# Two-layer diffusion backbone: where five modulation columns, the w2 loads and two weight casts of layer 1 stand in the program

## Chip, cores and metric

The kernel runs on one NeuronCore of a Trainium2 chip, in one launch. The metric is the device time of one execution in microseconds (us). Lower is better.

## The reference

A latent stream of 512 rows by 1,024 columns passes two layers; all arithmetic is f32.

```
for i in range(2):
    sh1, sc1, g1, sh2, sc2, g2 = split(silu(c) @ ada_w[i] + ada_b[i], 6)   # 6 vectors of 1024
    h = rms_norm(x, norm1_g[i]) * (1 + sc1) + sh1
    if i == 0:   # latent attention (8 heads) || Fourier mixing
        mix = concat(latent_attention(h @ a_w_in, context), fourier_mix(h @ a_w_in)) @ a_w_out
    else:        # conformer convolution || short gated convolution
        a, gate, sb, scc, sx = split(h @ b_w_in, 5 parts of 512)
        conf = depthwise_conv(a * sigmoid(gate), 31 taps) + bias
        conf = silu(group_layer_norm(conf, 4 groups))
        sc = sb * depthwise_conv(scc * sx, 3 taps)
        mix = concat(conf, sc) @ b_w_out
    x = x + g1 * mix
    h2 = rms_norm(x, norm2_g[i]) * (1 + sc2) + sh2
    x = x + g2 * ((silu(h2 @ w1[i]) * (h2 @ w3[i])) @ w2[i])        # inner width 2816
```

## The kernel before

Activations lie transposed in the on-chip buffer: tiles of 128 channels by 512 rows. A weight tile ("unit") is 128 by 1,024 f32 (512 KB; 448 KB for a part of w2). Every product with a weight is made of three matmuls on TensorE (`mm3`, L117 to L120): high part times high part, high times low, low times high. So a unit takes three steps: a DMA into a buffer `wraw` (three of them, `RB`), a cast to the high part `whi` on ScalarE (L95), and a subtraction that leaves the low part `wlo` (L96) on VectorE, or on GpSimd in layer 1's input projection (`lo_eng=G`). A unit of eight 128-wide blocks is 24 matmuls of 512 columns.

**Modulation columns.** The six vectors per layer are made in columns of 128 values. One column is a 512 KB DMA into a buffer `ada` (two of them, `AB`) and one multiply-and-sum on VectorE (L156 in `ada_tile`; L177 in `AdaJob.reduce`). The columns that are needed later wait in a list `bg` and are taken from it one by one: by `pump` in the plain part of layer 0's feed-forward, and by `pump_ahead` under the windows and the output tiles.

**Layer 0's output projection** is a list of steps between which `weave` spreads given columns.

**Layer 0's feed-forward** (`ffn_blocks(0, ...)`) goes over 22 inner blocks `f` in three segments of 8, 7 and 7 (`SEGS`). The first three blocks are plain (`proj` with `done`); the others are windows of small matmuls (L1212). At the end of each segment stand the output tiles: eight tiles `mt` of the product with w2, with `w2_ahead` for the weights of coming tiles, `pump_ahead` for a few modulation columns, and `add`, which puts the product into the residual (L327). The last segment's output tiles are called the turn here; layer 1's first input weights (`next_srcs`) and its first norm are prepared there. From the end of the plain part on, instructions are issued in the order of the program text. Elsewhere the framework's scheduler sets the order, save where a pair is pinned by `keep_in_program_order`.

**Layer 1's input projection** (`proj(in1, n1_1, done1, lo_eng=G, ..., pinned=3)`) has 20 units. Units 0 to 2 run interleaved, first on the left half of the rows, then on the right, while the norm's right half is prepared (`nrm.s2(1)`, `nrm.s3(1)`, whose last instructions on ScalarE are at L256). Units 3 to 19 follow one by one. `done1` takes each product: a gate's sigmoid on ScalarE (L1524), the product a * sigmoid on VectorE (L1530), and from it the 31-tap convolution of 128 channels. Its taps run on VectorE (L1474, on an accumulator in PSUM that ScalarE starts at L1471) and the last few as a scaling on ScalarE (L1478) with a sum on GpSimd (L1480). Each engine issues in order, so a weight's cast can stand behind a tap.

Of the kernel before, what the change touches and what calls it, by code (L numbers as in the profile page):

```python
# [60 lines left out]
def tile_dit(  # L61
# [914 lines left out]
    g1s = ada_jobs(0, "g1", 16, 8)  # L976
    s2s = ada_jobs(0, "s2", 24, 16)
    weave(pre, (g1s + s2s)[:SA0])
    weave(asteps, (g1s + s2s)[SA0:SA1])
# [23 lines left out]
    for x in END_ORDER.split():  # L1003
# [3 lines left out]
        else:  # L1007
            last.append(end[x])
    weave(last, (g1s + s2s)[SA1:])
    head0 = head_units(0)  # L1010
# [6 lines left out]
    def proj(srcs, nrm, done, first=3, lo_eng=None, head=(), mid=None, pinned=0):  # L1017
# [11 lines left out]
        for k in range(KT):  # L1029
            for u in range(first):  # L1030
                mm(u, k, 0, HS)
            if k == PH[0]:
                nrm.s1(1)
            if k == PH[1]:
                nrm.s2(1)
                nrm.s3(1)
        for u in range(first):
            for k in range(KT):
                mm(u, k, HS, S)
            done(u, pss[u])  # L1040
        for i in range(first, n):
            wh, wl = unit(srcs[i], D, lo_eng, i < first + pinned)
            if i == n - 1 and mid is not None:
                mid()
            p = ps()
            for k in range(KT):
                c = slice(k * P, (k + 1) * P)
                mm3(p, wh[:, c], wl[:, c], hh(k), hl(k), k == 0, k == KT - 1)
            done(i, p)
# [5 lines left out]
    def ffn_blocks(l, nrm, head, sq_next=None, make_next=None, next_srcs=(), next_head=None):  # L1055
# [30 lines left out]
        def done(i, p):  # L1086
# [11 lines left out]
            split(d[:, 0, :], d[:, 1, :], g)  # L1098
            if f < NPL - 1:
                pump(2)  # L1100
# [225 lines left out]
        for a, n in SEGS:  # L1326
# [3 lines left out]
            def w2src(mt):  # L1330
                return w2[l, mt, :, a:a + n, :]
# [32 lines left out]
            def w2_ahead(mt):  # L1364
                if mt + 3 < KT:
                    raw2.append(raw_unit(w2src(mt + 3), n * P))
                if mt + 2 < KT:
                    u = hilo()
                    split(u[0][:, :n * P], u[1][:, :n * P], raw2.pop(0)[:, :n * P])
                    wu.append(u)  # L1370
# [11 lines left out]
            for mt in range(full):  # L1382
# [4 lines left out]
                if not last and mt == KT - 2:  # L1387
                    run_prep(pn[4:])
                pump_ahead(((2, 1, 1, 1, 2, 0, 0, 0) if turn else (2, 2, 2, 2, 1 + (a == 0), 0, 0, 0))[mt])
                if turn and 0 < mt <= 3:  # L1390
# [39 lines left out]
    head1 = []  # L1430
    bg.extend(ada_jobs(0, "g2", 40, 8))
    bg.extend(ada_jobs(1, "s1", 0, 16))
# [121 lines left out]

    proj(in1, n1_1, done1, lo_eng=G, head=head1, pinned=3)
    g1b = mods[1, "g1"]
# [102 lines left out]
```

## Time and profile before

| | |
|---|---|
| device time, median of 3 runs | 1206.2 us (1205.64 to 1206.95) |
| device time of the profiled execution | 1205.26 us |
| its span in the trace | 1203.4 us |
| TensorE busy, share of the span | 1169.7 us, 97% |
| VectorE busy | 891.8 us, 74% |
| ScalarE busy | 517.8 us, 43% |
| GpSimd busy | 131.8 us, 11% |
| mean granted TensorE clock | 0.991 of full speed |

The span is the time from the first to the last instruction in the trace; the device time has 1.9 us more around it. A share is an average over stages with different limits, so what a change is worth is read in its own stage. In the trace PE is TensorE, PEld its weight load, DVE VectorE, ACT ScalarE, POOL GpSimd, and SP the engine that issues most DMAs; L with a number is a line of the kernel before. Matmuls overlap in the pipeline, so the pace is the distance between two starts, not the duration shown.

### The profile page before, as it was taken

Reading aid. Unit: us, or ns where it says so; the run is one execution under the profiler, and the core shown is the slowest. Engines: PE = TensorE matmul, PEld = TensorE weight load, DVE = VectorE, ACT = ScalarE, POOL = GpSimd, SP = SyncE. Lnnn points to the kernel's source line nnn. Section 1 sums busy time; section 2 is a strip of 40 time slices with the busy share of each in tenths; the row PEclk is TensorE's granted clock in tenths of the full one; section 3 lists DMA queues with packets and bytes.
Section 4 is the critical chain, followed back from the end, with each engine's and each line's share of the span. In section 5 each row is a group of like instructions: output and inputs, shape, how many; then the busy total and the mean of one; then the engine's idle time right before and its main releaser. Section 6 shows DMA issues by size and latency. Waiting matters only on the chain.

```text
span 1203.4 us, 18092 instructions
## 1 busy us (share of the span) xinstructions
PE 1169.7 (97%) x7128; PEld 1008.7 (84%) x7128; DVE 891.8 (74%) x1473; ACT 517.8 (43%) x879; POOL 131.8 (11%) x121
## 2 busy tenths in 40 slices
PE   8999999999999999999999879999999999999998
PEld 6777856569989899879988758878999889989997
DVE  7989877747887688678867779966877468757852
ACT  5545455535643244324433445433644235434530
POOL 1013300000000000000001187300000000000000
PEclk9999999999999999999999889999999999999999
DMA  9872033382478667766576032222068437726432
GB/s 345 300 290 88 1 109 102 108 268 97 135 217 249 233 195 224 219 219 203 159 255 197 18 123 88 80 96 88 28 175 210 123 90 179 210 73 159 113 100 94
DMA packets 56265, 188.34 MB, mean 157 GB/s; under 512 B 6130, under 2 KB 7026, under 8 KB 55923
## 3 DMA queue, kind: packets, MB, share of 16 engines
q1 hardware_dynamic: 51426, 169.88, 42.3%
q0 software_dynamic: 4752, 17.30, 8.5%
q8 instruction: 56, 0.92, 0.3%
q14 instruction: 31, 0.25, 0.1%
HBM read 185.06 MB, written 2.10 MB: 156 GB/s over the span
## 4 chain that ended last, share of the span: by engine, by line
PE 78%; DMA 9%; DVE 7%; ACT 2%; issue 2%; POOL 1%; SPq 0%; ACTq 0%; DVEq 0%; POOLq 0%
PE ps L1212 25%; PE ps L118 13%; PE ps L120 13%; PE ps L119 13%; DMA wraw<-in_w 5%; PE ps L921 2%; DMA ada<-in_ada 2%; PE ps L763 1%; DVE ada L177 1%; PE ps L636 1%; PE ps L926 1%; PE ps L906 1%; DVE s L96 1%; ACT whi L95 1%; PE ps L907 1%
## 5 line engine op out<-in xcount | busy, mean ns | idle before, releaser
L118 PE MATMUL ps<-s,whi 128*128 128x512 f32 (+1 forms) x758 | 283.1, 374 | 11.4 <-ACT whi L95 10.9
L1212 PE MATMUL ps<-s,whi 128*128 128x256 f32 x1584 | 287.4, 283 | 3.2 <-DVE t L1233 3.1
L120 PE MATMUL ps<-s,wlo 128*128 128x512 f32 (+1 forms) x758 | 279.1, 368 | 6.2 <-POOL wlo L96 3.9
L119 PE MATMUL ps<-s,whi 128*128 128x512 f32 (+1 forms) x758 | 278.3, 367 | 0.0
L1212 PEld LDWEIGHTS ps<-s,whi 128*128 128x128 f32 x1584 | 247.7, 192 | 4.7 <-DVE t L1233 3.8
L1212 PE MATMUL ps<-s,wlo 128*128 128x256 f32 x792 | 224.2, 283 | 0.4 <-DVE wlo L96 0.4
L95 ACT CAST whi<-wraw 128x1024 fp32r<-128x1024 f32 (+1 forms) x102 | 102.8, 1013 | 180.6 <-DMA wraw<-in_w 99.7
L118 PEld LDWEIGHTS ps<-s,whi 128*128 128x128 f32 x758 | 144.8, 191 | 37.2 <-ACT whi L95 13.4
L120 PEld LDWEIGHTS ps<-s,wlo 128*128 128x128 f32 x758 | 144.4, 190 | 34.0 <-POOL wlo L96 5.3
L119 PEld LDWEIGHTS ps<-s,whi 128*128 128x128 f32 x758 | 144.8, 191 | 22.8 <-issue 0.7
L1212 PEld LDWEIGHTS ps<-s,wlo 128*128 128x128 f32 x792 | 152.0, 192 | 0.6 <-DVE wlo L96 0.6
L96 DVE TENSOR_TENSOR wlo<-wraw,whi 128x1024 fp32r<-128x1024 f32 (+1 forms) x85 | 99.6, 1171 | 36.9 <-ACT whi L95 35.9
L327 DVE SCALAR_TENSOR_TENSOR x<-ps,m_g,x 128x512 f32<-128x512 f32 (+1 forms) x85 | 56.0, 666 | 79.6 <-PE ps L120 79.6
L95 ACT CAST whi<-s 128x1024 fp32r<-128x1024 f32 x65 | 67.7, 1046 | 73.1 <-PE ps L1212 31.8
L1139 POOL DMA_DIRECT2D s<-in_w x32 | 28.0, 875 | 559.9 <-DVE wlo L96 144.2
L96 DVE TENSOR_TENSOR wlo<-s,whi 128x1024 fp32r<-128x1024 f32 x65 | 78.9, 1221 | 6.3 <-ACT whi L95 4.0
L177 DVE CUSTOM_DVE_ANT_0 ada<-ada,scb,vec 128x1024 f32<-128x1024 f32 x52 | 66.2, 1280 | 11.6 <-DMA ada<-in_ada 11.6
L119 PE MATMUL ps<-s,s 128*128 128x256 f32 (+1 forms) x208 | 63.7, 309 | 0.4 <-DVE s L299 0.4
L120 PE MATMUL ps<-s,s 128*128 128x256 f32 (+1 forms) x208 | 63.2, 306 | 0.0
L118 PE MATMUL ps<-s,s 128*128 128x256 f32 (+1 forms) x208 | 61.3, 309 | 0.1
L1474 DVE SCALAR_TENSOR_TENSOR ps<-s,vec,ps 128x512 f32<-128x512 f32 x78 | 56.2, 751 | 2.1 <-ACT ps L1471 0.9
L1212 PE MATMUL ps<-s,u 128*128 128x256 f32 x396 | 52.9, 283 | 0.0
(285 smaller groups left out, 1903.9 us busy)
## 6 DMA issues: line engine op xcount, KB each, us to landing
ada<-in_ada SPq DMA_DIRECT2D x82, 512.0 KB, 3.9
s<-in_w SPq DMA_DIRECT2D x33, 768.0 KB, 5.7
wraw<-in_w SPq DMA_DIRECT2D x38, 512.0 KB, 4.8
s<-in_w SPq DMA_DIRECT2D x64, 256.0 KB, 4.3
s<-in_w POOLq DMA_DIRECT2D x32, 512.0 KB, 5.6
wraw<-in_w SPq DMA_DIRECT2D x32, 448.0 KB, 4.5
wraw<-in_w_in SPq DMA_DIRECT2D x17, 512.0 KB, 3.5
s<-in_ada SPq DMA_DIRECT2D x16, 512.0 KB, 6.7
```

What stands on the lines that cost most here:

```text
L95: i = A.copy(hi, src)
L96: j = (eng or V).tensor_sub(lo, src, f32(hi))
L118: T.matmul(o, wh, ah, start=start, stop=False)
L119: T.matmul(o, wh, al, start=False, stop=False)
L120: T.matmul(o, wl, ah, start=False, stop=stop)
L177: V.tensor_tensor_reduce(self.raw, self.raw, scb, 1.0, vc("ada_b", self.idx), ALU.mult, ALU.add, accum_out=self.dst)
L327: V.scalar_tensor_tensor(X[m][:, a:b], psum, gcol, X[m][:, a:b], ALU.mult, ALU.add)
L636: T.matmul(p[:, c], fst["fa"][:, g % 2, t, s * P:(s + 1) * P], fst["cs"][:, t, c], start=(t == 0), stop=(t == 3))
L921: T.matmul(p[64 * x:64 * x + 64, :], vh[t][:, 2 * j + x, :], ost["p", 2 * j + x, tp][:, s * S:(s + 1) * S], start=(t == 0), stop=(t == 5))
L1139: G.dma_start(s13, w[:, :D], accum_op=ALU.add)
L1212: T.matmul(o, w, b, start=start and kk == 0 and i == 0, stop=kk == 3 and i == 2, skip_group_check=True)
L1474: V.scalar_tensor_tensor(dst, cp[:, w:w + S], vec[:, o + w:o + w + 1], src, ALU.mult, ALU.add)
```

## The change

Five edits, all between layer 0's output projection and layer 1's input projection.

1. Five of the eight columns of layer 0's `g2` no longer wait in `bg`; `weave` spreads them in layer 0's output projection.
2. In the plain part, `done` takes two columns after block 0 alone, and no longer after block 1.
3. `w2_ahead` asks for the fourth and the fifth w2 unit together at the first output tile, so that each later request stands one tile earlier.
4. In the output tiles of the first two segments `pump_ahead` takes 2, 1, 2, 1, 2 columns in place of 2, 2, 2, 2, 1 (the first segment: 2). The turn's numbers stay.
5. In layer 1's input projection two units (3 and 4) are made right behind the norm, inside the loop over units 0 to 2, and pinned there. Before, units 3, 4 and 5 were pinned at the place of their use.

```
+    g2s = ada_jobs(0, "g2", 40, 8)
...
-    weave(last, (g1s + s2s)[SA1:])
+    weave(last, (g1s + s2s)[SA1:] + g2s[:5])
...
             if k == PH[1]:
                 nrm.s2(1)
                 nrm.s3(1)
+                ahead = [unit(srcs[i], D, lo_eng, True) for i in range(first, first + pinned)]
...
         for i in range(first, n):
-            wh, wl = unit(srcs[i], D, lo_eng, i < first + pinned)
+            wh, wl = ahead.pop(0) if ahead else unit(srcs[i], D, lo_eng)
...
-            if f < NPL - 1:
+            if f == 0:
                 pump(2)
...
             def w2_ahead(mt):
-                if mt + 3 < KT:
-                    raw2.append(raw_unit(w2src(mt + 3), n * P))
+                while 2 < len(raw2) + len(wu) <= mt + 4 and len(raw2) + len(wu) < KT:
+                    raw2.append(raw_unit(w2src(len(raw2) + len(wu)), n * P))
...
-                pump_ahead(((2, 1, 1, 1, 2, 0, 0, 0) if turn else (2, 2, 2, 2, 1 + (a == 0), 0, 0, 0))[mt])
+                pump_ahead(((2, 1, 1, 1, 2, 0, 0, 0) if turn else (2, 1, 2, 1, 2, 0, 0, 0))[mt])
...
-    bg.extend(ada_jobs(0, "g2", 40, 8))
+    bg.extend(g2s[5:])
...
-    proj(in1, n1_1, done1, lo_eng=G, head=head1, pinned=3)
+    proj(in1, n1_1, done1, lo_eng=G, head=head1, pinned=2)
```

The first place is ScalarE behind the norm of layer 1. The last line of L256 is the end of the norm; `t<-ps` is the gate's sigmoid, `ps<-s,vec` starts a convolution, `s<-s,vec` are ScalarE's taps, and `whi_` with `wraw_` is a weight's cast. Before:

```order
L256 ACTIVATE s_994_6170<-t_6322,m_s_2688 128x256
L1524 ACT_TABLE_LOAD
L1524 ACTIVATE t_6386<-ps_6243 128x512
L1471 ACTIVATE ps_6416<-s_1029_6412,vec 128x512
L1478 ACTIVATE s_1031_6417<-s_1029_6412,vec 128x512
L1478 ACTIVATE s_1009_6240<-s_1029_6412,vec 128x512 x2
L1524 ACTIVATE t_6453<-ps_6245 128x512
L95 CAST whi_6462<-wraw_6461 128x1024
L1471 ACTIVATE ps_6496<-s_1037_6492,vec 128x512
L1478 ACTIVATE s_1039_6497<-s_1037_6492,vec 128x512
L1478 ACTIVATE s_1009_6240<-s_1037_6492,vec 128x512 x3
L95 CAST whi_6512<-wraw_6511 128x1024
```

And with the change:

```order
L256 ACTIVATE s_994_6170<-t_6322,m_s_2703 128x256
L95 CAST whi_6327<-wraw_6326 128x1024
L95 CAST whi_6333<-wraw_6332 128x1024
L1526 ACT_TABLE_LOAD
L1526 ACTIVATE t_6398<-ps_6243 128x512
L95 CAST whi_6553<-wraw_6552 128x1024
L1473 ACTIVATE ps_6428<-s_1035_6424,vec 128x512
L1480 ACTIVATE s_1037_6429<-s_1035_6424,vec 128x512
L1480 ACTIVATE s_1009_6240<-s_1035_6424,vec 128x512 x2
L1526 ACTIVATE t_6465<-ps_6245 128x512
L95 CAST whi_6603<-wraw_6602 128x1024
L95 CAST whi_6648<-wraw_6647 128x1024
```

The casts of units 3 and 4 (the first two) now stand ahead of the sigmoid, and that of unit 5 ahead of the first convolution; two lines further on, L1473 starts the second convolution only behind a third cast, `whi_6692`.

The second place is GpSimd in the same stretch, from its last work for the norm (L148) on. Before, the sums of ScalarE's taps (L1480) stood between the low parts of units 3, 4 and 5:

```order
L148 TENSOR_TENSOR r_6278<-ms_6276,nhalf 128x2
L1480 TENSOR_TENSOR s_1031_6417<-s_1031_6417,s_1009_6240 128x512 x2
L96 TENSOR_TENSOR wlo_6463<-wraw_6461,whi_6462 128x1024
L1480 TENSOR_TENSOR s_1039_6497<-s_1039_6497,s_1009_6240 128x512 x3
L96 TENSOR_TENSOR wlo_6513<-wraw_6511,whi_6512 128x1024
```

With the change the same line numbers are two higher (L1482):

```order
L148 TENSOR_TENSOR r_6278<-ms_6276,nhalf 128x2
L96 TENSOR_TENSOR wlo_6328<-wraw_6326,whi_6327 128x1024
L96 TENSOR_TENSOR wlo_6334<-wraw_6332,whi_6333 128x1024
L96 TENSOR_TENSOR wlo_6554<-wraw_6552,whi_6553 128x1024
L1482 TENSOR_TENSOR s_1037_6429<-s_1037_6429,s_1009_6240 128x512 x2
L96 TENSOR_TENSOR wlo_6604<-wraw_6602,whi_6603 128x1024
```

Three low parts now stand ahead of the first sums.

The third place is the DMA issues of SP at the output tiles of the first segment (`wraw` is w2, `ada` a modulation column). Before:

```order
L114 DMA wraw_3692<-in_w 128x1024
L114 DMA wraw_3701<-in_w 128x1024
L174 DMA ada_3709<-in_ada 128x1024
L174 DMA ada_3712<-in_ada 128x1024
L114 DMA wraw_3740<-in_w 128x1024
L174 DMA ada_3748<-in_ada 128x1024
```

And with the change:

```order
L114 DMA wraw_3703<-in_w 128x1024
L114 DMA wraw_3712<-in_w 128x1024
L114 DMA wraw_3714<-in_w 128x1024
L174 DMA ada_3721<-in_ada 128x1024
L174 DMA ada_3725<-in_ada 128x1024
L114 DMA wraw_3753<-in_w 128x1024
L174 DMA ada_3760<-in_ada 128x1024
```

A third w2 load now stands ahead of the first two columns; it goes into the buffer that the preceding unit's split leaves. The turn's issues are moved in the same way.

## Rows read from the trace of the kernel before

**Rows 1.** The page, chain of work that ended last: shares by engine.

```profile
PE 78%; DMA 9%; DVE 7%; ACT 2%; issue 2%; POOL 1%; SPq 0%; ACTq 0%; DVEq 0%; POOLq 0%
```

**Rows 2.** Waits of PE: line, awaited line: us in total, times, longest.

```profile
PE ps L118 <- ACT whi L95: 10.9, 3, 6.0
PE ps L120 <- POOL wlo L96: 3.9, 2, 2.1
```

**Rows 3.** Timeline of PE, layer 1's input projection: start, us, instruction, [idle before].

```profile
682.87 0.79 PE L118 MATMUL ps<-s,whi 128*128 128x512 f32 x1 [3.25 <-ACT whi L95]
...
698.73 0.80 PE L118 MATMUL ps<-s,whi 128*128 128x512 f32 x1 [6.02 <-ACT whi L95]
...
706.42 0.39 PE L118 MATMUL ps<-s,whi 128*128 128x512 f32 x1
...
715.96 0.39 PE L118 MATMUL ps<-s,whi 128*128 128x512 f32 x1
```

**Rows 4.** Windows: stretch, length, busy us by engine, PEclk, DMA share, GB/s.

```profile
247.00:270.00 23.00, 23.00 (x120) 18.01 (x119) 14.73 (x17) 9.89 (x13) 1.06 (x1) 1.00 0.83 268
676.00:690.00 14.00, 8.99 (x44) 7.26 (x43) 9.76 (x13) 5.95 (x8) 4.85 (x3) 0.76 0.12 38
690.00:705.00 15.00, 6.87 (x21) 4.75 (x21) 12.15 (x19) 6.81 (x9) 9.12 (x6) 0.70 0.10 36
679.50:803.40 123.90, 110.38 (x480) 88.77 (x479) 103.74 (x146) 53.36 (x71) 64.28 (x41) 0.93 0.28 94
```

**Rows 5.** Timeline of ACT, layer 1's input projection.

```profile
676.04 1.28 ACT L1524 ACT_TABLE_LOAD   x1 [1.16 <-PE ps L120]
...
681.78 1.03 ACT L95 CAST whi<-wraw 128x1024 fp32r<-128x1024 f32 x1
693.61 0.78 ACT L1471 ACTIVATE ps<-s,vec 128x512 f32<-128x512 f32 x1 [10.79 <-DVE s L1530]
...
697.65 1.03 ACT L95 CAST whi<-wraw 128x1024 fp32r<-128x1024 f32 x1
```

**Rows 6.** Timeline of POOL, the same stretch.

```profile
683.45 2.35 POOL L96 TENSOR_TENSOR wlo<-wraw,whi 128x1024 fp32r<-128x1024 f32 x1
...
699.65 2.36 POOL L96 TENSOR_TENSOR wlo<-wraw,whi 128x1024 fp32r<-128x1024 f32 x1
```

**Rows 7.** Timeline of DVE, from the first convolution to the last product that awaits it.

```profile
679.57 9.46 DVE L1474 SCALAR_TENSOR_TENSOR ps<-s,vec,ps 128x512 f32<-128x512 f32 x12 [0.91 <-ACT ps L1471]
...
714.87 0.69 DVE L1530 TENSOR_TENSOR s6a<-ps,t 128x512 f32<-128x512 f32 x1 [5.43 <-PE ps L120]
...
803.36 0.75 DVE L327 SCALAR_TENSOR_TENSOR x<-ps,m_g,x 128x512 f32<-128x512 f32 x1 [1.18 <-PE ps L120]
```

**Rows 8.** Timeline of DVE and PE, end of the plain part.

```profile
330.59 1.28 DVE L156 CUSTOM_DVE_ANT_0 ada<-ada,scb,vec 128x1024 f32<-128x1024 f32 x1 [1.62 <-DMA ada<-in_ada]
...
333.07 0.39 PE L1212 MATMUL ps<-s,wlo 128*128 128x256 f32 x1 [0.44 <-DVE wlo L96]
...
337.67 0.50 PE L1212 MATMUL ps<-s,whi 128*128 128x256 f32 x2 [1.71 <-DVE t L1233]
```

**Rows 9.** Timeline of PE, output tiles of the first and the second segment.

```profile
424.23 0.50 PE L120 MATMUL ps<-s,wlo 128*128 128x512 f32 x1 [0.53 <-DVE wlo L96]
...
521.68 0.50 PE L120 MATMUL ps<-s,wlo 128*128 128x512 f32 x1 [0.39 <-DVE wlo L96]
```

**Rows 10.** Timelines of SP's queue and PE, the turn.

```profile
622.16 1.53 SPq L174 DMA_DIRECT2D ada<-in_ada  x2
623.79 0.38 SPq L114 DMA_DIRECT2D wraw<-in_w  x1
...
642.88 0.39 PE L118 MATMUL ps<-s,whi 128*128 128x256 f32 x1 [1.60 <-ACT whi L95]
```

**Rows 11.** The page: the columns' group on DVE, and the loads from issue to landing.

```profile
L177 DVE CUSTOM_DVE_ANT_0 ada<-ada,scb,vec 128x1024 f32<-128x1024 f32 x52 | 66.2, 1280 | 11.6 <-DMA ada<-in_ada 11.6
...
ada<-in_ada SPq DMA_DIRECT2D x82, 512.0 KB, 3.9
```

## The prediction

> **What bounds the kernel now.** I read the chain of the work that ended last first: 78% of it is TensorE, the rest is mostly DMA and VectorE [rows 1]. So there is little to win but the places where TensorE stands still, and the next view is the list of TensorE's waits. Its two largest entries belong together: 10.9 us for a weight's high part from ScalarE and 3.9 us for a low part from GpSimd [rows 2]. The timeline puts nearly all of both into layer 1's input projection: TensorE idles 3.25 us ahead of unit 3 and 6.02 us ahead of unit 4 [rows 3].
>
> The waits are not the whole loss there. While TensorE stands, the granted clock falls: 0.76 of full speed over 676 to 690 us and 0.70 over 690 to 705 [rows 4], so that matmuls run at the lower of the two levels (1.2 in place of 2.4 GHz) for some microseconds behind each wait. I measure the whole from end to end. Unit 3's first matmul waits until 682.87 and could have started 3.25 us earlier, at 679.62. At 706.42 stands matmul 13 of unit 4, behind 24 of unit 3 and 12 of unit 4. The pace without a wait is (715.96 - 706.42) / 42 = 0.227 us, the 42 being the matmuls between those two rows [rows 3]. So 36 matmuls need 8.2 us and took 26.8: **18.6 us** are lost.
>
> Why were the weights late? ScalarE's cast of unit 3 came at 681.78, that of unit 4 at 697.65 [rows 5], and GpSimd's low parts at 683.45 and 699.65 [rows 6]. ScalarE is not full: ahead of unit 4's cast it waited 10.79 us at 693.61 to start the second convolution, for VectorE's product [rows 5], which itself needs TensorE's unit 3. It is a ring: TensorE waits for the cast, the cast stands behind a convolution that waits for TensorE.
>
> **The change, part by part.**
>
> *Edit 5, the two casts behind the norm.* ScalarE has 1.16 us of idle time behind the norm, up to 676.04, where it waits for unit 0 [rows 5]. The casts go there: from 674.9 (676.04 less 1.16), 1.03 us each, to 676.9. The sigmoid then starts some 0.8 us late, and with it VectorE's first tap, at 680.4 in place of 679.57 [rows 7]. GpSimd, now without sums ahead, makes a low part in 2.35 us [rows 6]: unit 3's from 675.9 to 678.3, unit 4's to 680.6, unit 5's to 683.0. TensorE needs unit 3 at 679.6, unit 4 at 679.6 + 24 x 0.227 = 685.1, unit 5 at 690.5. None is late, so the ring is cut and up to 18.6 us come back.
>
> What is late next is VectorE. From the first tap to the residual at 803.36 that closes the first step of layer 1's output projection it is busy 103.74 of 123.9 us [rows 4, 7]. If it never waited, it would be there at 680.4 + 103.7 = 784.1; TensorE without the loss is there at 803.36 - 18.6 = 784.8. Both ends coincide, so any wait that VectorE keeps costs TensorE too. One I expect: ScalarE must make three casts ahead of the second convolution's start, the last into a buffer that GpSimd releases with unit 5's low part, at 683.0; a load takes 3.9 us by the nearest row [rows 11] and the cast 1.03, so ScalarE gets on at 688, some 2 us after VectorE could use it. I take **16.0 us** for this edit, 18.6 less 2.6; the bounds are 18.6 and 11 (rival 1).
>
> *Edits 1 and 2.* Block 1's two columns leave the plain part: 2 x 1.28 us of VectorE, and a 1.62 us wait for the second one's load [rows 8]. Right behind them TensorE waits 0.44 and 1.71 us for VectorE [rows 8]; both go, with about 0.35 us of slower restarts behind them (estimated from the 0.50 us of the matmul pair at 337.67 where the usual is 0.40): 2.5 us (bounds 1.5 and 2.5). In exchange five columns, 5 x 1.28 = 6.4 us of VectorE, go into layer 0's output projection. VectorE is busy 14.73 of 23 us there and TensorE 23.00 of 23 [rows 4]: the 8.3 us of idle VectorE time cover them, in pieces, and I cost them at nothing. Their five loads of 512 KB need 9.8 us at that stretch's 268 GB/s, with the DMA engines busy 0.83 [rows 4], so weights may come later; the bound is 2 us, and without any cover 6.4.
>
> *Edits 3 and 4.* Under the output tiles of the first segment TensorE waits once 0.53 us for a low part, and in the second three times 0.39, 0.39 and 0.34; the first of each stands for them [rows 9]. Each leaves 0.17 us of slower pace behind. One column less in the second and the fourth tile gives VectorE 1.28 us [rows 11], and the weights are asked for a tile earlier: I count all back, 0.7 + 1.6 = 2.3 us (lower bound 0).
>
> In the turn the table of columns is the same and only the requests move. There two columns were issued at 622.16 and the w2 load at 623.79, behind them [rows 10]; now a w2 load goes ahead of two columns, and VectorE, in order, reaches the columns first. If a 448 KB load delays them by what it moves at 268 GB/s, about 1.7 us, and part of that is slack, VectorE's loop gets 1 us later; against that stands TensorE's 1.60 us wait for a weight at 642.88 [rows 10], which an earlier request may shorten. I take a loss of 1.0 us (bounds +2.5 and -2.5). The Trainium skill (DMA: Bandwidth & Descriptors, Queues, rings and completion order) says that descriptors of one ring are consumed in ring order, which speaks against asking for w2 first; by it the loss would be the 1.7 us whole, and rows 10 show only issues, no landing order that could decide.
>
> **Sum.** 16.0 + 2.5 - 0 + 2.3 - 1.0 = 19.8 us. The profiled execution took 1205.26 us, its span 1203.4; so 1185.5 us for one like it, and from the median of 1206.2, which is 0.9 us higher, **1186.4 us**.
>
> **Rivals.**
>
> 1. *The convolution becomes the bound.* VectorE has no microsecond to spare by the sum above; the point from which it decides is 2.6 us of waits in all. If GpSimd is slower with three low parts in a row, say 4.7 us each (twice the 2.35 of rows 6), the third buffer is free at 690, its cast ends at 695, and the second convolution starts 7 us later than I count. Edit 5 then gives back 9 to 12 us in place of 16.0, and the time is 1190.5 to 1193.5. For it: VectorE's thin margin. Against it: the low part at 683.45 took 2.35 us while VectorE was in the midst of its taps, and the one at 699.65 took 2.36 [rows 6, 7]. The Trainium skill (SBUF — State Buffer, SBUF: two separate sides) gives it a mechanism: VectorE and GpSimd share a port pair as an exclusive lock when a VectorE instruction reads two operands from this buffer, which the norm's do; those two rows show no such lock beside taps, which read PSUM and one operand.
> 2. *Only unit 3's wait goes.* If a later unit has to wait as unit 4 does now, because its load, asked for only when GpSimd frees a buffer, lands late, half of the loss returns: 6.02 + 2 + some 3 us of low clock, 11 us, so 1197 (1194 to 1203). It decides if a load takes over 13 us: unit 6's buffer is asked for at 678.3 and the unit is needed at 695.9, and the landing is 3.9 us by rows 11. Against it: that margin.
> 3. *Slower.* In each of 15 output tiles with columns (five per segment) the w2 load stands ahead of the columns on SP's queue and itself waits for a buffer. If VectorE's columns came later by a whole load, 3.9 us [rows 11], less the tile's slack, taken as 1.2, each tile would cost 2.7 us: 15 x 2.7 = 40, less the 18.5 of the other places is 21.5 slower, 1228. It decides from 18.5 / 15 = 1.2 us per tile. For it: VectorE already waits 11.6 us for columns in all [rows 11]. Against it: each request moves ahead of a column by one place, and the tiles of the first two segments lose columns.
>
> **How the numbers follow.** The forecast (1182 to 1190) 0.66; rival 1 (1190 to 1194) 0.20; rival 2 (1194 to 1203) 0.09; rival 3 0.04; a better end than all of these 0.01. The range 1182 to 1194 leaves out 0.14; its lower end is all of the 18.6 and the turn's better bound in part (18.6 + 2.5 + 2.3 + 0.5 = 23.9), its upper end rival 1 with the bound of 2 us in layer 0's output projection. This kernel's measurement can tell 0.2%, 2.4 us, from no change. Faster by more 0.94, within it 0.02 (the end of rival 2's tail), slower 0.04.
>
> **What would show it.** Edit 5 right: no idle time of TensorE ahead of units 3 and 4, a granted clock of 1.00 over the whole input projection, casts directly behind L256, and VectorE over 95% busy from its first tap to the close of the output projection's first step, at about 787 in before's count, less what earlier edits gave. Rival 1: the same casts, but TensorE waits for VectorE's mean or merge in the output projection. Rival 2: a wait for ScalarE at unit 5 or later. Edits 1 to 4: no waits like those of rows 8 and 9, and in the turn either a longer wait than 1.60 us (my loss) or a shorter one. Rival 3: more idle VectorE time ended by a column's load, in every tile. The prediction fails most cheaply if VectorE holds up the mean of a convolution, or if layer 0's output projection, which I cost at nothing, starts to wait for its weights.

## The result, and the profile after

The changed kernel takes 1186.34 us (median of 3 runs, 1184.24 to 1187.83) against 1206.2 before: a ratio of 0.983 (95% interval 0.981 to 0.986). The prediction was 1186.4. That the median fits to a tenth is partly luck, as the parts below show; a second set of runs beside the kernel before on another chip gave 1188.35 with the same ratio, 0.983 (0.981 to 0.985). The profiled execution took 1184.24 us, its span 1182.4, 21.0 less than before's.

The chain of the work that ended last now has 84% of TensorE where [rows 1] had 78%:

```profile
PE 84%; DVE 4%; DMA 4%; issue 3%; POOL 2%; ACT 2%; SPq 0%; POOLq 0%; DVEq 0%; ACTq 0%
```

The list of TensorE's waits (line, awaited line: us in total, times, longest) has lost both entries of [rows 2]; the 2.6 us for a cast are the turn's 1.54 and one of 1.04 us in the second segment's tiles. A new one stands near the top, for a merge (L1489) ahead of a convolution's mean:

```profile
PE ps L343 <- ACT crow L134: 3.2, 1, 3.2
PE ps L1503 <- DVE s L1489: 2.8, 1, 2.8
PE ps L118 <- ACT whi L95: 2.6, 2, 1.5
PE ps L120 <- DVE wlo L96: 1.4, 3, 0.6
```

In the timeline of PE, unit 3 (675.59) and unit 4 (681.04) of layer 1's input projection start without any idle time, where [rows 3] had 3.25 and 6.02 us; the distance between the two, 5.45 us, is 24 matmuls at full pace:

```profile
675.59 0.40 PE L118 MATMUL ps<-s,whi 128*128 128x512 f32 x1
...
681.04 0.39 PE L118 MATMUL ps<-s,whi 128*128 128x512 f32 x1
...
716.64 1.12 PE L1503 MATMUL ps<-s,ones 128*128 128x512 f32 x2 [2.80 <-DVE s L1489]
```

The windows (stretch, length, busy us of PE, PEld, DVE, ACT and POOL, PEclk, DMA share, GB/s) show a granted clock of 1.00 where [rows 4] had 0.76 and 0.70. They also show GpSimd busy nearly without a break (41.52 of 45 us over 675 to 720), which no row of before had:

```profile
672.00:686.00 14.00, 14.00 (x78) 12.23 (x77) 8.85 (x13) 12.09 (x16) 13.90 (x7) 1.00 0.41 130
686.00:701.00 15.00, 15.00 (x68) 12.40 (x67) 15.00 (x24) 6.65 (x10) 14.69 (x10) 1.00 0.44 141
675.00:720.00 45.00, 42.20 (x188) 34.40 (x187) 40.17 (x58) 24.65 (x34) 41.52 (x25) 1.00 0.40 132
```

ScalarE's timeline has the two casts right behind the norm (L256), ahead of the table load, where [rows 5] had them at 681.78 and 697.65. The third cast before the second convolution waits 1.45 us for its load, so L1473 starts at 683.61; the last row is for later:

```profile
670.10 0.91 ACT L256 ACTIVATE s<-t,m_s 128x256 fp32r<-128x256 f32 x2 [1.06 <-DVE t L251]
670.91 1.98 ACT L95 CAST whi<-wraw 128x1024 fp32r<-128x1024 f32 x2
672.92 1.28 ACT L1526 ACT_TABLE_LOAD   x1
...
682.66 1.05 ACT L95 CAST whi<-wraw 128x1024 fp32r<-128x1024 f32 x1 [1.45 <-DMA wraw<-in_w_in]
683.61 0.78 ACT L1473 ACTIVATE ps<-s,vec 128x512 f32<-128x512 f32 x1
...
690.16 0.72 ACT L1480 ACTIVATE s<-s,vec 128x512 f32<-128x512 f32 x1 [3.90 <-POOL s L1482]
```

And GpSimd's has three low parts in a row, 2.38 us each, as against 2.35 and 2.36 in [rows 6]:

```profile
672.03 7.14 POOL L96 TENSOR_TENSOR wlo<-wraw,whi 128x1024 fp32r<-128x1024 f32 x3 [8.41 <-ACT whi L95]
679.13 2.66 POOL L1482 TENSOR_TENSOR s<-s,s 128x512 f32<-128x512 f32 x2
```

**Where the time came from.** All kernels here issue nearly the same work in nearly the same order, so the start of the same instruction in two traces gives the length of a stage. Markers: the third L954, at the end of layer 0's attention (235.38 in the trace of before; line numbers are before's), the first, ninth and fourteenth L1233 (337.20, 494.64, 607.88), TensorE's last L241 of layer 1's first norm (663.60), the second group mean's L241 (767.16) and the last L1233 (1153.17). The stage between two is the difference of their starts, in us:

| kernel | output projection 0, norm, plain part | windows and tiles, segment 1 | tiles 2, windows 3 | turn, norm | input projection | rest |
|---|---|---|---|---|---|---|
| before | 101.82 | 157.44 | 113.24 | 55.72 | 103.56 | 386.01 |
| changed | 100.40 | 156.30 | 112.30 | 55.68 | 87.84 | 384.62 |
| changed, run 9 | 104.06 | 156.46 | 110.91 | 56.29 | 89.24 | 384.62 |

The changed kernel's first trace wins 15.7 us in the input projection, 1.4 up to the first window, 1.1 and 0.9 in the two segments and nothing in the turn. Another 1.4 us lie in the rest, which no edit touches. Some 1.0 of them is a wait in layer 1's first window, which took 1.41 us in before's trace, 0.44 in this one and between 0.40 and 1.55 in the others, with or without the change. Nor is the 1.1 us of the first segment shown to come from the change: run 1 below, which has neither edit 3 nor edit 4, takes the same 156.30 us there. The second trace of the same kernel loses 2.2 us ahead of the first window instead of winning 1.4. That stage is the part that the prediction had wrong.

### The profile page after: what moved, and what is told of

Its sections match the earlier page's. It is cut to its first block, busy times and chain, and to the rows that moved or that the text cites. A ratio compares the mean times of both kernels' runs of the same rounds, so it can differ in the third digit from the quotient of the medians.

```text
span 1182.4 us, 18092 instructions
## 1 busy us (share of the span) xinstructions
PE 1163.4 (98%) x7128; PEld 1007.3 (85%) x7128; DVE 887.3 (75%) x1473; ACT 517.1 (44%) x879; POOL 130.9 (11%) x121
## 4 chain that ended last, share of the span: by engine, by line
PE 84%; DVE 4%; DMA 4%; issue 3%; POOL 2%; ACT 2%; SPq 0%; POOLq 0%; DVEq 0%; ACTq 0%
PE ps L1214 26%; PE ps L118 15%; PE ps L120 15%; PE ps L119 15%; PE ps L921 2%; DMA wraw<-in_w 2%; DMA s<-in_w 1%; PE ps L763 1%; POOL wlo L96 1%; PE ps L636 1%; PE ps L906 1%; ACT whi L95 1%; PE ps L907 1%; PE ps L908 1%; PE ps L926 1%
## 5 line engine op out<-in xcount | busy, mean ns | idle before, releaser
L177 DVE CUSTOM_DVE_ANT_0 ada<-ada,scb,vec 128x1024 f32<-128x1024 f32 x49 | 62.5, 1281 | 7.6 <-DMA ada<-in_ada 7.5
```

Source lines behind the costliest of these rows:

```text
L177: V.tensor_tensor_reduce(self.raw, self.raw, scb, 1.0, vc("ada_b", self.idx), ALU.mult, ALU.add, accum_out=self.dst)
```

## The experiments

Twelve kernels ran, in three groups, each group on one chip beside the kernel before (1208.46, 1205.63 and 1207.43 us there; so the ratios are what to compare).

| run | median us | ratio to before, 95% interval |
|---|---|---|
| 1 casts alone | 1191.47 | 0.985 (0.984 to 0.987) |
| 2 without the casts | 1201.36 | 0.994 (0.992 to 0.995) |
| 3 first cast only | 1194.95 | 0.987 (0.984 to 0.991) |
| 4 no pins | 1194.70 | 0.988 (0.987 to 0.990) |
| 5 later mean | 1188.23 | 0.985 (0.981 to 0.989) |
| 6 columns earlier | 1185.38 | 0.982 (0.979 to 0.985) |
| 7 requests as before | 1188.12 | 0.984 (0.980 to 0.987) |
| 8 columns as before | 1185.79 | 0.983 (0.979 to 0.987) |
| 9 changed again | 1188.35 | 0.983 (0.981 to 0.985) |
| 10 fewer taps | 1188.68 | 0.984 (0.983 to 0.986) |
| 11 columns in the attention | 1180.12 | 0.977 (0.976 to 0.979) |
| 12 more in the attention | 1193.22 | 0.988 (0.987 to 0.990) |

And the stages of their traces, as above:

| run | outproj 0 to plain | segment 1 | tiles 2, windows 3 | turn, norm | input proj. | rest |
|---|---|---|---|---|---|---|
| 1 | 102.69 | 156.30 | 112.68 | 55.73 | 89.36 | 385.46 |
| 2 | 99.63 | 156.91 | 111.86 | 55.84 | 104.52 | 385.81 |
| 3 | 106.74 | 156.31 | 110.30 | 55.87 | 95.67 | 385.78 |
| 4 | 99.51 | 156.53 | 112.02 | 69.75 | 84.32 | 385.58 |
| 6 | 100.04 | 156.48 | 110.30 | 55.98 | 87.88 | 384.85 |
| 7 | 103.52 | 156.30 | 113.05 | 55.60 | 87.82 | 385.54 |
| 8 | 100.28 | 156.30 | 112.82 | 52.12 | 89.45 | 385.09 |
| 11 | 100.04 | 156.51 | 110.29 | 50.79 | 89.51 | 385.40 |
| 12 | 101.45 | 156.47 | 110.30 | 50.79 | 89.49 | 385.09 |
| 5 | 101.00 | 156.38 | 110.30 | 55.77 | – | – |
| 10 | 104.79 | 156.30 | 112.85 | 55.79 | – | – |

(Runs 5 and 10 change the order around the means, so their last two stages don't compare and are left out.)

**Run 1, the casts alone.** The kernel before with edit 5 only:

```
+                ahead = [unit(srcs[i], D, lo_eng, True) for i in range(first, first + pinned)]
...
-            wh, wl = unit(srcs[i], D, lo_eng, i < first + pinned)
+            wh, wl = ahead.pop(0) if ahead else unit(srcs[i], D, lo_eng)
...
-    proj(in1, n1_1, done1, lo_eng=G, head=head1, pinned=3)
+    proj(in1, n1_1, done1, lo_eng=G, head=head1, pinned=2)
```

Expected: 

> Edit 5 alone on the kernel before (two casts behind the norm, pinned 2 in place of 3). Theory A, a ring at ScalarE (a cast stood behind a convolution that waited for TensorE's own product): the stages before are untouched, so the in-projection's share comes alone, 15.7 us by the two traces: 1206.2 - 15.7 = 1190.5 (1189 to 1192), no wait ahead of units 3 and 4, and a wait of some 3 us for VectorE's merge at the first mean. Rival B, the earlier loads and the relieved VectorE of edits 1 to 4 carry a good part of it: 1194 or more, and waits for weights stay.

Measured: 17.0 us less than before on that chip (1208.46 - 1191.47), of which the input projection shows 14.2 and the rest 0.6. No wait at units 3 and 4, 2.86 us at the mean. Theory A holds; the earlier loads are not needed for it. The run is also a control for the other edits, which it lacks: against before's trace it takes 0.9 us more up to the first window, and 1.1 and 0.6 us less in the two segments. So much one execution can differ from another there, and differences of that size in the table above are not of themselves an edit's.

**Run 2, all but the casts.** The changed kernel with these places undone.

Expected: 

> Edits 1 to 4 without edit 5. Theory A: only the stages before layer 1 gain, by the two traces -0.6 + 2.0 + 1.15 + 0.95 = 3.5 us, so 1202.7 (1201 to 1204), and TensorE waits 3.25 and 6.02 us ahead of units 3 and 4 as before, at the lower clock behind each. Rival B: 1198 or less, and these waits shrink.

Measured: 7.1 us less than before on that chip, more than the 3.5 of theory A; by its trace's stages up to the turn it is 4.0 (2.2 + 0.5 + 1.4 - 0.1); the rest lies within the spread of before's runs on that chip (1205.08 to 1210.20), of which there is no trace. Runs 1 and 2 together win 24.1 us by these medians, more than the 19 to 20 of the whole change, so that group's median of before is probably high. The waits stand as in [rows 3], on theory A's side (timeline of PE):

```profile
678.41 0.50 PE L118 MATMUL ps<-s,whi 128*128 128x512 f32 x1 [3.25 <-ACT whi L95]
...
694.89 0.79 PE L118 MATMUL ps<-s,whi 128*128 128x512 f32 x1 [6.03 <-ACT whi L95]
```

**Run 3, the first cast only.** Unit 4 is made and pinned at its place of use again:

```
-            wh, wl = ahead.pop(0) if ahead else unit(srcs[i], D, lo_eng)
+            wh, wl = ahead.pop(0) if ahead else unit(srcs[i], D, lo_eng, pinned and i < first + 3)
...
-    proj(in1, n1_1, done1, lo_eng=G, head=head1, pinned=2)
+    proj(in1, n1_1, done1, lo_eng=G, head=head1, pinned=1)
```

Expected: 

> The changed kernel, but only unit 3's cast stands behind the norm; that of unit 4 is back at its place behind the second convolution's start. Theory A: unit 3's wait is gone, unit 4's is as before, since its cast still waits for a product of unit 3: some 5 to 6 us for the high part, 2.1 for the low part and 3 of low clock, less the 2.8 us wait for the merge, which this delay covers: 1186.3 + 8 = 1194 (1192 to 1197). Rival C, unit 4 was late only because unit 3 was: both waits go, 1186 to 1188.

Measured: unit 3 does not wait, unit 4 waits as before to a hundredth (timeline of PE):

```profile
692.15 0.79 PE L118 MATMUL ps<-s,whi 128*128 128x512 f32 x1 [6.02 <-ACT whi L95]
...
695.49 0.80 PE L120 MATMUL ps<-s,wlo 128*128 128x512 f32 x1 [2.12 <-POOL wlo L96]
```

The input projection takes 95.67 us, 7.8 more than the changed kernel's 87.84 (8 were expected). So each of the two casts has its own turn of the ring, and the change needs both. This is shown. The run's four times lie 8.7 us apart (1189.74 to 1198.42), and the trace, from one of the longer ones, loses 5 us long before, behind layer 0's output projection; run 6 is about that.

**Run 4, no pins.** Without `ahead` and without a pin the scheduler puts the casts of units 3 to 7 among the norm's instructions:

```
-    proj(in1, n1_1, done1, lo_eng=G, head=head1, pinned=2)
+    proj(in1, n1_1, done1, lo_eng=G, head=head1)
```

Expected: 

> The changed kernel, but with no pin and nothing made ahead in layer 1's input projection: the scheduler then puts the casts of units 3 to 7 among the norm's instructions, ahead of its last ones. Theory A (any place ahead of the convolutions cuts the ring): no wait ahead of units 3 and 4; the first convolution starts up to 0.85 us sooner and the second 2 us sooner, GpSimd's low part ahead of the norm's power costs TensorE some 1 us: 1185 to 1188. Rival D, the place right behind the norm matters: casts that wait for loads hold up the norm, TensorE waits 3 us or more for the norm's right half, 1190 or more.

Measured: rival D. The input projection is the fastest of all, 84.32 us (the floor that the prediction worked out is 103.56 - 18.6 = 85.0), with no wait at the means. But the turn and the norm take 69.75 us, 14.1 more. ScalarE's timeline shows the largest part of the reason: a cast waits for a weight buffer that TensorE still reads, and the norm's copy (L245) stands behind it (at 660.81, in the changed kernel at 653.33); TensorE in its turn waits for the norm.

```profile
659.86 1.05 ACT L95 CAST whi<-wraw 128x1024 fp32r<-128x1024 f32 x1 [4.65 <-PE ps L119]
660.81 0.36 ACT L245 COPY rb<-ps 128x256 f32<-128x256 f32 x1
```

So being early is half of it: the place right behind the norm's last line is what the change has right. Whether a third unit would still fit there no run shows.

**Run 5, the means one unit later.**

```
-        jobs.append(lambda: later(2, lambda: ln(j)))
+        jobs.append(lambda: later(3, lambda: ln(j)))
```

Expected: 

> The changed kernel, but each convolution's group mean (two matmuls) comes one unit later in TensorE's order (a delay of 3 in place of 2 steps). Theory A: TensorE's 2.8 us wait for VectorE's merge at the first mean is all that VectorE holds up, since the other three means did not wait; it goes, and nothing takes its place: 1186.3 - 2.8 = 1183.5. Rival E, VectorE is the bound from the first tap to the end of the output projection's first step (its busy time alone ends at 784 in before's count): the wait comes back at a later mean or residual, 1185.5 to 1188.

Measured: rival E's side, no gain (0.985, interval 0.981 to 0.989). The wait for the merge is gone, and one of 2.24 us for ScalarE's square (L1506) stands 26 matmuls behind (timeline of PE):

```profile
727.18 1.05 PE L241 MATMUL ps<-ones,t 128*128 128x2 f32 x8 [2.24 <-ACT t L1506]
```

**Run 10, four taps fewer.** It was to say whether the work of VectorE sets that limit; four of the first convolution's VectorE taps are left out:

```
-        for w in range(1, nd):
+        for w in range(1 if j else 5, nd):
```

Expected: 

> The changed kernel, with four of the VectorE taps of the first convolution left out (the output lacks them): some 4 x 0.7 us of VectorE work less. Theory E (VectorE bounds the input projection and the output projection's first step): the wait for the merge at the first mean shrinks from 2.8 to 0.3 us or less, nothing takes its place, and it ends 2.5 us sooner than the run above. Rival, a fixed chain of ScalarE and GpSimd sets the merge: the wait stays over 2 us, and the time is the same.

Measured: no gain beside run 9 (1188.68 and 1188.35). The wait at the first mean shrinks to 0.66 us, one of 2.58 us follows at the square. First the timeline of PE, then of DVE, then of ACT:

```profile
713.85 1.10 PE L1503 MATMUL ps<-s,ones 128*128 128x512 f32 x2 [0.66 <-DVE s L1489]
723.01 1.05 PE L241 MATMUL ps<-ones,t 128*128 128x2 f32 x8 [2.58 <-ACT t L1506]
```

```profile
711.10 0.76 DVE L1476 SCALAR_TENSOR_TENSOR ps<-s6a,vec,ps 128x512 f32<-128x512 f32 x1 [3.33 <-ACT ps L1473]
```

```profile
705.07 0.73 ACT L1480 ACTIVATE s<-s6a,vec 128x512 f32<-128x512 f32 x1 [3.78 <-POOL s L1482]
706.44 0.72 ACT L1480 ACTIVATE s<-s6a,vec 128x512 f32<-128x512 f32 x1 [0.65 <-POOL s L1482]
```

This does not say that VectorE's work sets no limit, for the run moved more than the taps. The convolution's list of jobs is four shorter, so the first mean stands a whole unit, 24 matmuls, earlier in TensorE's order. And the trace reaches the input projection 4.8 us later, so that the same stretch is not 675 to 720 but this:

```profile
679.80:724.80 45.00, 41.77 (x187) 33.89 (x186) 39.37 (x57) 25.36 (x35) 39.96 (x25) 0.99 0.39 129
```

VectorE is busy 39.37 us in it, in place of 40.17. Counted from the same point, the merge ends 7.7 us sooner than in the changed kernel (it starts at 713.02 less 4.8, in place of 715.91), while GpSimd's sums stand where they stood; so the merge does follow VectorE's work, against the rival. But theory E's gain does not come either: VectorE waits 3.33 us for the start of the third convolution, which ScalarE reaches late because its scaled copies (L1480) wait for GpSimd's sums (L1482). In the changed kernel's trace the two engines take turns at being full (GpSimd is the fifth busy time, VectorE the third):

```profile
675.00:710.00 35.00, 35.00 (x159) 29.11 (x158) 30.17 (x45) 22.59 (x31) 34.29 (x21) 1.00 0.38 121
710.00:745.00 35.00, 32.20 (x146) 25.92 (x146) 33.90 (x50) 15.32 (x20) 21.73 (x15) 1.00 0.31 105
```

So which of them is the limit behind the casts stays open: no run took GpSimd's sums away, and none took VectorE's taps away without moving the mean. The scheduler also put the remaining taps in another order, so the run does not price a tap.

**Run 6, four columns from the output projection into the attention.**

```
-SA0, SA1, SC, PU, RB, TB, AB = 1, 20, 15, 6, 3, 5, 2
+SA0, SA1, SC, PU, RB, TB, AB = 1, 24, 15, 6, 3, 5, 2
```

Expected: 

> The changed kernel, but four columns more are made in layer 0's attention and so four fewer in its output projection (five there, as one more than before). Theory F, edit 1's loads fill the DMA queues at 270 to 286 us, so that the first feed-forward weights land late by an amount that changes from run to run (0.6 us lost in the trace of the changed kernel, 5 in that of the third experiment): the DMA share at 274 to 278 falls from 0.98 to under 0.3, those weights land in 4 us, the loss goes, the runs lie within 2.5 us of each other, 1185 to 1187. Rival G, the attention has no room on VectorE for 4 x 1.28 us: 1188 to 1191.

Measured: theory F in the trace, though the DMA share falls to 0.57 and not under 0.3, and the spread of the times is 4.0 us (1182.61 to 1186.65), not 2.5. The attention has the room: no wait is new there. The windows of 274 to 278 us, of before, the changed kernel and run 6 (DMA share is the number before the last):

```profile
274.00:278.00 4.00, 4.00 (x21) 3.34 (x20) 2.60 (x4) 3.35 (x6) 0.00 (x0) 1.00 0.05 22
```

```profile
274.00:278.00 4.00, 4.00 (x19) 3.33 (x18) 4.00 (x6) 3.42 (x5) 0.00 (x0) 1.00 0.98 364
```

```profile
274.00:278.00 4.00, 4.00 (x19) 3.32 (x18) 1.22 (x2) 3.35 (x6) 0.00 (x0) 1.00 0.57 227
```

Before, the DMA engines had room there when the feed-forward's first weights were asked for; with edit 1 they are full. The landing of the weights asked for between 272 and 284 us (min, median, max) in run 3 and in run 6; in before it was 3.6/3.9/4.1, in the changed kernel 5.0/5.2/7.6, in run 9 4.5/7.8/8.3:

```profile
DMA to landing us min/median/max: 4.4/8.1/8.7
```

```profile
DMA to landing us min/median/max: 3.3/3.6/3.8
```

The weights were not asked for later: the first of them was requested at 279.02 us in before and at 276.16 to 277.64 in the nine traces with edits 1 and 2. What a late landing costs stands in run 3. ScalarE's cast waits for the load, VectorE's low part for the cast, and behind the low part stand the residual and the square for the norm's sum, for which TensorE waits. The granted clock falls behind it (window of 295 to 300 us, PEclk 0.51), so that the stage takes 6 to 7 us more than in the changed kernel's first trace and run 4's, which have no wait (first the timeline of ACT, then of DVE and PE, then the window):

```profile
288.04 1.05 ACT L95 CAST whi<-wraw 128x1024 fp32r<-128x1024 f32 x1 [4.17 <-DMA wraw<-in_w]
```

```profile
289.12 1.22 DVE L96 TENSOR_TENSOR wlo<-wraw,whi 128x1024 fp32r<-128x1024 f32 x1 [4.29 <-ACT whi L95]
293.12 1.01 PE L241 MATMUL ps<-ones,acc 128*128 128x2 f32 x4 [2.78 <-DVE acc L336]
```

```profile
295.00:300.00 5.00, 5.00 (x26) 5.00 (x26) 1.30 (x3) 0.00 (x0) 1.06 (x1) 0.51 0.00 0
```

Of nine traces with edits 1 and 2 (the changed kernel, runs 2 to 5 and 7 to 10), six have this wait, between 0.17 and 3.00 us; before and runs 1, 6, 11 and 12 have none. The median landing of these weights is 5.2 to 8.1 us in all nine, and 3.6 to 4.1 us in before and runs 1, 6 and 11.

The traces also show what tells the nine apart. The columns on SP's queue push back two loads for the feed-forward's first window (tile `s6b`, asked for at 254.79 us in before and at 268.91 in the changed kernel), and with them a third one on GpSimd's queue that is added to these two. First before, then the changed kernel, then run 3 (timeline of POOL):

```profile
261.33 1.06 POOL L1139 DMA_DIRECT2D s6b<-in_w x1 [123.55 <-DMA s6b<-in_w]
```

```profile
278.40 1.05 POOL L1141 DMA_DIRECT2D s6b<-in_w x1 [140.95 <-PE ps L120]
```

```profile
277.92 1.05 POOL L1141 DMA_DIRECT2D s6b<-in_w x1 [140.08 <-ACT t L335]
```

So it now falls together with the request for the second of the late weights (278.27 in the changed kernel, 279.24 in run 3). In the five traces with a wait of 1.22 us or more it is issued first, by 0.04 to 1.4 us, and that weight takes 7.5 to 8.7 us; in the other four it is issued 0.05 to 0.3 us behind, and the weight takes 4.9 to 5.5. That this order decides is read off nine traces; no run moved that load alone.

**Runs 7 and 8, edit 3 and edit 4 undone.** `w2_ahead` as before, and the table of columns as before.

Expected: 

> The changed kernel with edit 3 undone: w2 is asked for one unit at a time as before. Prediction's term: the turn gains 1.0 us, since columns no longer stand behind a w2 load. By the two traces the turn changes by less than 0.2 us. In the first two segments' tiles the columns of edit 4 carry the gain (theory A): they lose at most 0.5 us, 1186 to 1187, and the 1.04 us wait for a cast at 509 us goes. Rival H, the earlier requests carry it: both segments lose their 1.15 and 0.95 us, 1188.4.

Expected: 

> The changed kernel with edit 4 undone: the tiles of the first two segments take 10 and 9 columns again in place of 8 and 8, so the list is empty three columns sooner and the turn makes three fewer. Theory A: the two segments lose 1.15 + 0.95 us, the turn (VectorE 5.6 us per tile against TensorE's 4.8) gains up to 2: 1186 to 1188. Rival I, the columns under the tiles cost nothing once w2 is asked for sooner: no loss in the segments, and the turn's gain makes it 1184 to 1185.5.

Measured: neither time differs from the changed kernel's by more than the intervals. In the stages the first segment takes 156.30 us with either edit alone, and as much in run 1 with neither, so no run shows that its 1.1 us belong to them. The second segment takes 113.05 and 112.82 with one of them, and 113.24 and 112.68 in before and run 1 with neither; with both it takes between 110.30 and 112.85 in ten traces, 110.30 in five of them. So the pair wins up to 2.9 us there, and sometimes next to nothing. The turn hardly changes with the requests (55.60 against 55.68 and 56.29). It does with three columns fewer: 52.12, 3.6 us less, more than the 2 expected. There the wait for a cast is 0.20 us in place of 1.54 and the clock stays at 1.00. Of that, run 8 gives back 0.5 to 1.9 us in the second segment, where a low part comes 1.79 us late. Theory A and rival I foretold times too close to each other for its four runs (1183.08 to 1191.17) to choose.

**Runs 9, 11 and 12, a better place for the columns.** Run 9 is the changed kernel. Run 11 makes layer 0's 32 columns of `g1`, the second norm's vectors and `g2` ahead of its output projection, and four of layer 1's in it:

```
-SA0, SA1, SC, PU, RB, TB, AB = 1, 20, 15, 6, 3, 5, 2
+SA0, SA1, SC, PU, RB, TB, AB = 1, 32, 15, 6, 3, 5, 2
...
+    s1n = ada_jobs(1, "s1", 0, 16)
...
-    weave(asteps, (g1s + s2s)[SA0:SA1])
+    weave(asteps, (g1s + s2s + g2s)[SA0:SA1])
...
-    weave(last, (g1s + s2s)[SA1:] + g2s[:5])
+    weave(last, s1n[:4])
...
-    bg.extend(g2s[5:])
-    bg.extend(ada_jobs(1, "s1", 0, 16))
+    bg.extend(s1n[4:])
```

Run 12 goes on (`SA1` 40, eight of `s1n` in the attention, none in the output projection).

Expected: 

> The changed kernel once more, beside the next three on one chip: a ratio to the kernel before of 0.983 (0.981 to 0.986), about 20 us less. Theory F also expects that its own runs lie 3 to 5 us apart, and that a trace which loses time does so at the norm behind layer 0's output projection (289 to 293 us).

Expected: 

> All of layer 0's columns are made in its attention (12 more than in the changed kernel), its output projection takes four of layer 1's, as many as it had before the change, and the list is 7 shorter, so that the turn makes none. Theory F: the weights behind the output projection land in 4 us, no wait at 289 to 293 (0.6 us or more won); the turn's waits of 1.54 and 0.43 us go with part of the slow pace behind them (1.6 us with three columns fewer, up to 3 with seven): 3 us less than the run above. Rival G, VectorE has no room in the attention for 12 x 1.28 = 15 us: TensorE waits there, no gain or a loss.

Expected: 

> The attention also takes eight columns of layer 1 (20 more than in the changed kernel, 26 us of VectorE, busy there 21.5 of 30 us by the windows), layer 0's output projection none. Theory F: as the run above or 0.5 us better, if the attention holds them (31 us of 180 to 300 are free only in part); rival G decides here first: waits of TensorE for VectorE between 100 and 240 us, 2 us or more slower than the run above.

Measured: run 11 is faster than both kernels, 0.977 (0.976 to 0.979) against 0.983 (0.981 to 0.985) for the changed kernel on the same chip, 8.2 us by the medians where 3 were expected. The stages against run 9 say where: 4.0 us up to the first window (the weights land in 4.0 us again, and no wait stands at the norm), 0.6 in the second segment and 5.5 in the turn, which makes no columns now and has none of the waits of [rows 10]. Of the 5.5 us, 3.0 are three waits of run 9's turn, and some 1.7 by estimate (0.17 of 10 us) the low clock, which goes with them: PEclk is 0.83 over 640 to 650 us in run 9, and with it in the changed kernel's first trace; here it is 1.00 (first that trace, then run 11):

```profile
640.00:650.00 10.00, 9.44 (x65) 9.24 (x65) 7.70 (x15) 1.89 (x4) 0.97 (x2) 0.83 0.78 233
```

```profile
640.00:650.00 10.00, 10.00 (x87) 10.00 (x86) 4.29 (x11) 2.53 (x6) 1.32 (x9) 1.00 0.01 2
```

In run 12 the attention is full and rival G decides: the stretch up to 235 us in before's count takes 12.1 us more, in waits like this one.

```profile
214.02 0.89 PE L892 MATMUL ps<-identr,s 128*97 128x128 f32 x4 [3.70 <-DVE s L884]
```

Run 9's trace, of its longest execution (1189.11 us), has a 2.37 us wait at the norm behind layer 0's output projection, where theory F expects the loss. Its five runs lie 6.5 us apart (1182.58 to 1189.11), more than the 3 to 5 expected.

## Why the prediction was right, point by point

- **The bound and the mechanism** (a ring of cast, convolution and TensorE's own product): right, and shown by runs 1 to 3. With both casts moved the waits go; with one, the other's stays at 6.02 us.
- **The term of 16.0 us for edit 5**: 15.7 in the changed kernel's first trace, 14.3 in its second and 14.2 in run 1. The 2.6 us that I took off came, as a wait of 2.80 at the first mean. Its size was in part luck: at the second convolution's start, from which I had worked it out, VectorE waited 1.04 us and not 2 (timeline of DVE below). The lower values are the granted clock, which falls behind this wait in some executions (last section).
- **"What is late next is VectorE"**: right as to the wait; that VectorE is full was too strong. It was to be over 95% busy from its first tap to the close of the output projection's first step. In the changed kernel's first trace that stretch is 105.60 us long and VectorE is busy for 97.84 of them, 93%. Its work, which I had put at 103.7 us by the row of the kernel before, took less, so both ends did not coincide. What I left out of the count is GpSimd, which over 675 to 710 us is the fuller of the two. Run 10 does not settle which of them is the limit. The rows are one of DVE's timeline and one window:

```profile
684.49 9.32 DVE L1476 SCALAR_TENSOR_TENSOR ps<-s,vec,ps 128x512 f32<-128x512 f32 x14 [1.04 <-ACT ps L1473]
```

```profile
676.40:782.00 105.60, 102.58 (x465) 83.82 (x464) 97.84 (x143) 48.45 (x65) 59.64 (x40) 1.00 0.31 103
```

- **The term of 2.5 us for edits 1 and 2, with the five columns at nothing**: the step that failed. The change won 1.4 us in one trace and lost 2.2 in the other; over the nine traces with both edits this stage takes 102.2 us on average (99.51 to 106.74) against 101.82 before. The waits of [rows 8], 0.44 and 1.71 us, do go but for one of 0.36 us in the changed kernel (run 1, without these edits, has 0.59 and 1.70), and the four traces with at most 0.17 us of wait at the norm win 1.4 to 2.3 us, near the 2.5. VectorE has the room that I counted, though none is left at 274 to 278 us; the loads do not. I named them (9.8 us of transfers, the weights may come later), set 2 us as the bound, and took 0; run 3's trace is 6 to 7 us longer in this stage than those without a wait. What the columns delay is the feed-forward's first weights, whose late cast holds up a norm.
- **2.3 us for the tiles**: 2.1 and 3.3 in the two traces, but the 1.0 to 1.1 of the first segment stands in run 1 too, without the edits. Only the second segment's share, 0.9 and 2.3 us, can be theirs. So the number fits partly by luck.
- **A loss of 1.0 us in the turn**: nothing in the first trace, 0.6 lost in the second; and by runs 7 and 8 the requests' order is worth less than 1 us there and the columns' number 3.6 us. The rule of the Trainium skill that I weighed against it (DMA: Bandwidth & Descriptors, Queues, rings and completion order) gave 1.7 us; no run shows that much.
- **The sum**: too much by 1 to 5 us for edits 1 and 2, too little by 0.4 to 1 for the turn, and 1.4 us in layer 1 that belong to no edit. These cancel in the median, and that is luck.
- **Rivals**: rival 1 (the convolution as the bound) showed its wait at the size I had counted in, not more. GpSimd's low parts took 2.38 us in a row; the lock of the Trainium skill (SBUF — State Buffer, SBUF: two separate sides) is not seen beside taps, and the norm's instructions with two operands, of which the prediction spoke, did not run beside these three low parts, since the norm had ended. Rival 2, a later unit that waits because its load lands late, did not come: behind unit 4 TensorE waits for no weight in the changed kernel's input projection. Run 3 makes unit 4 wait by its cast instead, at 7.8 us. Rival 3, VectorE starved in every tile, did not come: VectorE's wait for columns fell from 11.6 to 7.5 us.

## What to carry to other kernels

Where an engine issues in order, look for a preparation that stands behind work which itself waits for the engine being fed: it costs its wait and the low clock behind, and it goes by moving a short instruction to the last place where its engine idles anyway, not simply earlier (run 4). A column of work moved onto an engine with idle time still brings its loads; here they pushed others back, and the weights that were asked for next landed late. So look at the DMA share right behind the stretch, and prefer a stretch where both are low (run 11). One trace of a kernel whose loads are tight is one draw: compare two before a term of a few us is believed, and see whether a kernel without the edit shows the same gain, as run 1 does here in the first segment.

## What the hardware showed

The same wait of TensorE, 2.80 to 2.86 us at the first mean, lowers the granted clock in some executions and not in others. The wait ends at 716.64 us in the changed kernel's first trace, and the clock is 1.00 up to 720 (the row of 675 to 720 above) and from 720 to 725. It ends at 720.17 in the second trace, and the clock is 0.69 right behind it:

```profile
720.00:725.00 5.00, 5.00 (x28) 4.28 (x27) 5.00 (x9) 2.28 (x3) 0.82 (x1) 1.00 0.21 79
```

```profile
720.00:725.00 5.00, 4.83 (x13) 3.27 (x14) 5.00 (x9) 0.30 (x1) 1.73 (x1) 0.69 0.58 204
```

The input projection then takes 87.8 us (changed kernel, runs 6 and 7) or 89.2 to 89.5 (runs 1, 8, 9, 11 and 12), so this alone makes 1.4 to 1.7 us between executions. What decides it no run shows.
